# Ordering the rotary queries' split behind two evictions in a four-layer attention trunk

## The chip, the core and the metric

The kernel runs on one core of a Trainium2 chip. The metric is the device time of one execution in microseconds (us); several executions are timed and the median is taken. One further execution is recorded by the hardware profiler.

The engines are called as the profile calls them: PE is TensorE (matmul), PEld its weight load, DVE is VectorE, ACT is ScalarE, POOL is GpSimd, and SP is SyncE, which here only issues transfers.

## The reference

The reference is a decoder trunk of four layers over 256 positions of width 2048, batch 1, all in float32. The layers' token mixers are latent attention (layers 0 and 3), a sparse attention with an indexer (layer 1) and a sliding window (layer 2). The change concerns the latent layers:

```python
c_q, c_kv, k_rope, mq, gate = _split(h @ w_in, [A_Q_LORA, A_KV_LORA, A_ROPE, MEM_WIDTH, BRANCH_WIDTH])
q = (_rmsnorm(c_q, q_norm) @ w_uq).reshape(B, S, A_HEADS, A_NOPE + A_ROPE)      # 16 heads, 128 + 64
kv = (_rmsnorm(c_kv, kv_norm) @ w_ukv).reshape(B, S, A_HEADS, A_NOPE + A_V)     # 16 heads, 128 + 128
q_nope, q_rope = q[..., :A_NOPE], _rope(q[..., A_NOPE:])
k_nope, v = kv[..., :A_NOPE], kv[..., A_NOPE:]
k_rope = _rope(k_rope)                                                          # one for all heads
...
s = (jnp.einsum('bqhd,bkhd->bhqk', qn, k_nope) + jnp.einsum('bqhd,bkd->bhqk', qr, k_rope)) * scale
p = jax.nn.softmax(jnp.where(causal, s, NEG_INF), axis=-1)
return jnp.einsum('bhqk,bkhd->bqhd', p.astype(v.dtype), v)
```

Each layer also attends to 256 memory rows, multiplies the concatenated heads by SiLU of a gate, and adds an output projection to the residual.

## The kernel before

**Numbers in two parts.** A float32 operand is held as a high part, rounded to the format that PE multiplies, and a low part, the difference. A split is one ACT copy (line 58, in the helper `copy_act`) and one DVE subtraction. A product of two split operands is three matmuls: high by high, high by low, low by high. Weights come in pieces of 128 x 1024 by SP's transfers (`wr`), and are split into `wh` (ACT, line 58) and `wl` (DVE, line 72); these splits are kept in the order of the pieces.

**One latent layer.** `Latent.first` makes the latent queries and keys. Then `Latent.project(g)` runs for four groups g of four heads each, followed by `Latent.attend` (scores, softmax, values) and the gate. Over the two latent layers that makes eight groups. Within one group, `project` does, in the order of writing:

1. The rotary queries, `acc_qr`: products by `rows_by`, rotated on DVE, transposed by blocks (`qrT` L457), written to DRAM by POOL (`placed` L463) and read back by four POOL transfers into the tile `qrR` (L473).
2. The latent queries without rotation, `acc_qn`, in two halves of two heads, by `columns_by`. Each half's accumulator is evicted by `head_parts`: an ACT copy of the high part (`qn`, L58), a DVE subtraction (`zl`, L316) and a DVE addition (`qn`, L317).
3. The latent keys, `acc_kn`, in two halves, evicted in the same way. The second half lies in two small accumulators (`apart`), so that `head_parts` takes its other branch: two ACT copies, then L312 and L313 on DVE for each of two heads.
4. The values, `acc_va`, by `rows_by` in two steps of 12 matmuls, s = 0 and s = 2; L266, L267 and L268 are the three products.
5. The function `rotary`, called from a hook of `rows_by` after the matmuls of step s = 0: it splits `qrR` into the tile `qrT`, an ACT copy (L842, seen as L58) and a DVE subtraction on 64 partitions (L843).

`attend` then multiplies the queries by the keys, `sp<-kn,qn`, and the rotary queries by the rotary keys, `sp<-kr,qrT` (both L870).

**Accumulators and buffers.** The large accumulators share two places (`bufs=2`), taken in turn: `acc_qr`, the two halves of `acc_qn`, the first half of `acc_kn`, `acc_va`. So `acc_va` gets the place of the second half of `acc_qn`, as soon as its L317 has ended. The tiles `qrR`, the two `qn` and the two `kn` share five places (`PQ`); `wh` and `wl` have three each.

**What sets the order.** The order of writing is not the order of the engines' queues. A planner goes through a simulated timeline at compile time and puts on each engine the instruction that is ready by its own estimates. Two devices bind it: `tc.keep_in_program_order(x)` keeps marked instructions of an engine in the order of writing among themselves, and `with tc.issue_after(ins)` puts every instruction of the block that runs on the engine of `ins` behind `ins` in that queue. On the chip each queue then runs in the planned order, and an instruction that waits holds up what stands behind it.

## Time and profile before

| | before |
|---|---|
| median of three runs | 2533.45 us (2532.8 to 2538.79) |
| profiled execution: its own time | 2536.98 us |
| profiled execution: span from the first to the last instruction | 2535.2 us |
| mean granted PE clock | 0.998 of full speed |
| busy: PE, DVE, ACT, POOL | 2507.9, 1804.6, 1417.0, 386.0 us |
| busiest pieces of DVE and ACT: the weights' L72, the weights' L58 | 1027.5, 891.3 us |
| moved by transfers | 595.13 MB, mean 235 GB/s |

A line of the timeline gives the start (us from the start of the span), the duration (us), the engine, the line of the kernel, the operation, the tile written and the tiles read, shapes and types, and how many instructions the line merges; a bracket gives the time that the engine stood idle before it and what ended that time. A row of the view by stretches gives the stretch, its length, PE's busy time and number of instructions, the mean granted PE clock, the busy share of the 16 DMA engines and what they moved in GB/s.

The eight groups' `acc_va` start at 535, 623, 713, 804 us (layer 0) and 2114, 2201, 2288, 2377 us (layer 3).

### The profile page before, as it was taken

The page shows a single profiled execution, that of the slowest core. Times are in us where ns is not written, and L with a number is a line of the kernel's source. Part 1 is how long each engine was busy: PE and PEld are TensorE (multiplying, and loading weights), DVE is VectorE, ACT ScalarE, POOL GpSimd, SP SyncE. Part 2 cuts the span into 40 slices and gives each one's busy share as a digit, 9 for nine tenths or more (in the row PEclk, how much of TensorE's full clock was granted, in tenths as well). Part 3 has the DMA queues.
Part 4 walks back from the last instruction along what each step waited for, and adds up shares of the span by engine and source line. Part 5 has one row for each costly group of instructions (what it writes and reads, how often), then busy time and mean ns, then how long its engine had stood idle before and what let it go on. Part 6 is the DMA issues. An engine that isn't in the chain of part 4 may idle for free.

```text
span 2535.2 us, 37192 instructions
## 1 busy us (share of the span) xinstructions
PE 2507.9 (99%) x12868; PEld 2142.0 (84%) x12868; DVE 1804.6 (71%) x3039; ACT 1417.0 (56%) x2240; POOL 386.0 (15%) x615
## 2 busy tenths in 40 slices
PE   8999999999999999999999999999999999999998
PEld 7888888888888888988888888887889888888887
DVE  6555556777767676778888775887887677767677
ACT  6454545554555455656666555666665555545554
POOL 1000001111111110012222201222220111011110
PEclk9999999999999999999999999999999999999999
DMA  9888888977878766679899677999985897788874
GB/s 314 263 280 291 271 261 261 248 202 206 221 201 218 219 190 193 202 230 281 258 281 259 211 213 210 271 270 252 265 235 160 259 240 208 204 225 219 243 207 149
DMA packets 451741, 595.13 MB, mean 235 GB/s; under 512 B 79376, under 2 KB 270496, under 8 KB 450400
## 3 DMA queue, kind: packets, MB, share of 16 engines
q1 hardware_dynamic: 411792, 470.76, 63.5%
q0 software_dynamic: 38752, 121.08, 16.7%
q8 instruction: 102, 1.67, 0.3%
q10 hardware_dynamic: 1008, 0.91, 0.1%
q14 instruction: 87, 0.71, 0.1%
HBM read 535.25 MB, written 69.96 MB: 239 GB/s over the span
## 4 chain that ended last, share of the span: by engine, by line
PE 95%; DMA 2%; DVE 1%; ACT 1%; issue 1%; POOL 0%; SPq 0%; ACTq 0%; DVEq 0%; POOLq 0%
PE acc_mq L290 5%; PE acc_g L290 5%; PE acc_gr L268 4%; PE acc_gr L267 4%; PE acc_gr L266 4%; PE acc_wo L266 4%; PE acc_wo L268 4%; PE acc_wo L267 4%; PE acc_qn L290 3%; PE acc_wo L241 3%; PE acc_wo L239 3%; PE acc_wo L240 3%; PE acc_mq L292 2%; PE acc_g L292 2%; PE acc_mk L267 2%; PE acc_mk L268 2%
## 5 line engine op out<-in xcount | busy, mean ns | idle before, releaser
L72 DVE TENSOR_TENSOR wl<-wr,wh 128x1024 fp32r<-128x1024 f32 (+2 forms) x860 | 1027.5, 1197 | 556.4 <-ACT wh L58 547.8
L58 ACT ACTIVATE wh<-wr 128x1024 fp32r<-128x1024 f32 (+2 forms) x860 | 891.3, 1038 | 840.1 <-PE acc_gr L268 99.4
L267 PE MATMUL acc_gr<-wl,xT 128*128 128x512 f32 x512 | 199.6, 390 | 0.0
L266 PE MATMUL acc_gr<-wh,xT 128*128 128x512 f32 x512 | 199.5, 390 | 0.0
L268 PE MATMUL acc_gr<-wh,xT 128*128 128x512 f32 x512 | 199.5, 390 | 0.0
L266 PE MATMUL acc_wo<-wh,y 128*128 128x512 f32 x432 | 168.8, 391 | 0.5 <-DVE x L1202 0.5
L268 PE MATMUL acc_wo<-wh,y 128*128 128x512 f32 x432 | 168.4, 390 | 0.0
L267 PE MATMUL acc_wo<-wl,y 128*128 128x512 f32 x432 | 168.4, 390 | 0.0
L290 PE MATMUL acc_g<-xT,wh 128*128 128x512 f32 x512 | 162.3, 395 | 0.0
L290 PE MATMUL acc_mq<-xT,wh 128*128 128x512 f32 x512 | 161.8, 396 | 0.0
L577 POOL DMA_DIRECT2D pL<-turn x192 | 120.5, 634 | 210.6 <-DMA turn<-T 92.4
L241 PE MATMUL acc_wo<-wh,y 128*128 128x512 f32 x320 | 124.9, 390 | 0.2 <-DVE y L62 0.2
L240 PE MATMUL acc_wo<-wl,y 128*128 128x512 f32 x320 | 124.9, 390 | 0.1
L239 PE MATMUL acc_wo<-wh,y 128*128 128x512 f32 x320 | 125.0, 390 | 0.0
L1202 DVE TENSOR_TENSOR x<-x,acc_wo 128x1024 f32<-128x1024 f32 x92 | 111.4, 1211 | 16.1 <-PE acc_wo L268 11.4
L290 PE MATMUL acc_qn<-cT,wh 128*128 128x512 f32 x384 | 120.6, 395 | 0.0
L292 PEld LDWEIGHTS acc_g<-xT,wl 128*128 128x128 f32 x512 | 96.0, 188 | 21.7
L292 PEld LDWEIGHTS acc_mq<-xT,wl 128*128 128x128 f32 x512 | 95.1, 188 | 21.1
L267 PEld LDWEIGHTS acc_gr<-wl,xT 128*128 128x128 f32 x512 | 96.2, 188 | 19.3 <-DVE wl L72 0.2
L266 PEld LDWEIGHTS acc_gr<-wh,xT 128*128 128x128 f32 x512 | 96.2, 188 | 19.1
L268 PEld LDWEIGHTS acc_gr<-wh,xT 128*128 128x128 f32 x512 | 96.2, 188 | 19.1
L266 PE MATMUL acc_mv<-wh,mT 128*128 128x512 f32 x256 | 100.7, 394 | 7.3 <-ACT wh L58 7.3
(339 smaller groups left out, 5777.5 us busy)
## 6 DMA issues: line engine op xcount, KB each, us to landing
wr<-in_w_out_dram SPq DMA_DIRECT2D x192, 512.0 KB, 4.9
wr<-in_w_in_a_dram SPq DMA_DIRECT2D x176, 512.0 KB, 4.9
wr<-in_w_mem_kv_dram SPq DMA_DIRECT2D x128, 512.0 KB, 5.8
wr<-in_w_in_b_dram SPq DMA_DIRECT2D x116, 512.0 KB, 4.5
wr<-in_w_in_c_dram SPq DMA_DIRECT2D x104, 512.0 KB, 4.9
wr<-in_w_uq_dram SPq DMA_DIRECT2D x288, 128.0 KB, 3.8
turn<-T POOLq DMA_DIRECT2D x40, 384.0 KB, 5.1
tab<-flat POOLq DMA_DIRECT2D x8, 1536.0 KB, 11.4
```

Source lines behind the costliest of these rows:

```text
L58: return nc.scalar.activation(o, i, AF.Copy, scale=scale)
L72: two = nc.vector.tensor_sub(lo, src, f32(hi))
L239: nc.tensor.matmul(accs[c][:, t], xh, wh[:, at], start=first, stop=False)
L240: nc.tensor.matmul(accs[c][:, t], xh, wl[:, at], start=False, stop=False)
L241: nc.tensor.matmul(accs[c][:, t], xl, wh[:, at], start=False, stop=last)
L266: nc.tensor.matmul(acc[:, t, :n], xh, wh[:, at], start=first, stop=False)
L267: nc.tensor.matmul(acc[:, t, :n], xh, wl[:, at], start=False, stop=False)
L268: nc.tensor.matmul(acc[:, t, :n], xl, wh[:, at], start=False, stop=last)
L290: nc.tensor.matmul(acc[j], wh[:, at[j]], q[:, :, kt % 4, :], start=first, stop=False)
L292: nc.tensor.matmul(acc[j][:, 0, :], wl[:, at[j]], q[:, 0, kt % 4, :], start=False, stop=last)
L577: nc.gpsimd.dma_start(f32(self.raw)[j * 32:(j + 1) * 32, :].rearrange("p (i r) -> p i r", r=r), bass.AP(tensor=d.tensor, offset=d.offset + ...
L1202: nc.vector.tensor_add(xs, xs, acc)
```

## The change

`head_parts` returns its last ACT copy and its last DVE addition. `project` keeps those of the second half of the queries (`ahead`) and of the second half of the keys (`begun`), and `rotary` puts its two instructions behind them, each on its own engine. The hook that calls `rotary` moves from step 0 of the values to step 2.

```diff
         if isinstance(acc, list):
             at = [(dst[:, :, j], z[:, j], acc[j]) for j in range(2)]
             for d, zj, q in at:
-                copy_act(d[:, 0], q[:, 0, :])
+                one = copy_act(d[:, 0], q[:, 0, :])
             for d, zj, q in at:
                 nc.vector.tensor_sub(zj, q[:, 0, :], f32(d)[:, 0])
-                nc.vector.tensor_add(d[:, 1], zj, q[:, 1, :])
-            return
-        copy_act(dst[:, 0], acc[:, :, 0, :])
+                two = nc.vector.tensor_add(d[:, 1], zj, q[:, 1, :])
+            return one.ins, two.ins
+        one = copy_act(dst[:, 0], acc[:, :, 0, :])
         nc.vector.tensor_sub(z, acc[:, :, 0, :], f32(dst)[:, 0])
-        nc.vector.tensor_add(dst[:, 1], z, acc[:, :, 1, :])
+        two = nc.vector.tensor_add(dst[:, 1], z, acc[:, :, 1, :])
+        return one.ins, two.ins
...
                 q = act.tile([P, 2, 2, S], F32R, name="qn", tag="pq", bufs=PQ)
-                head_parts(q, acc)
+                ahead = head_parts(q, acc)
                 qn.append(q)
 
             def rotary():
                 r4 = raw[:].rearrange("p (t m b) -> p m t b", m=4, b=32)
-                tc.keep_in_program_order(copy_act(quads(qr), r4))
-                nc.vector.tensor_sub(quads(qr)[64:], r4[64:], quads(f32(qr))[64:])
+                with ExitStack() as held:
+                    for ins in ahead + begun:
+                        held.enter_context(tc.issue_after(ins))
+                    tc.keep_in_program_order(copy_act(quads(qr), r4))
+                    nc.vector.tensor_sub(quads(qr)[64:], r4[64:], quads(f32(qr))[64:])
...
                 k = act.tile([P, 2, 2, S], F32R, name="kn", tag="pq", bufs=PQ)
-                head_parts(k, acc)
+                begun = head_parts(k, acc)
                 kn.append(k)
             acc = rows_by(self.cT[3:], 4, wkv, 0, (g * 1024, 4, 256, A_NOPE, A_NOPE), "va",
-                          {0: [rotary]})
+                          {2: [rotary]})
```

## The prediction

> **What bounds the kernel now.** I read the page first, for the engine that fills the span and for the chain that ended last.

> ```profile
> span 2535.2 us, 37192 instructions
> PE 2507.9 (99%) x12868; PEld 2142.0 (84%) x12868; DVE 1804.6 (71%) x3039; ACT 1417.0 (56%) x2240; POOL 386.0 (15%) x615
> PE 95%; DMA 2%; DVE 1%; ACT 1%; issue 1%; POOL 0%; SPq 0%; ACTq 0%; DVEq 0%; POOLq 0%
> ```

> TensorE (PE) fills the span but for 27 us, and the chain runs through it. So only time in which PE stands still, or runs slowly, can be won. The view of waits, for PE, says where it stands (waited for: us in total, times, longest).

> ```profile
> PE acc_va L266 <- DVE qn L317: 7.5, 7, 2.9
> PE acc_mv L266 <- ACT wh L58: 7.3, 1, 7.3
> PE acc_va L266 <- ACT kn L58: 1.2, 1, 1.2
> ```

> The first weights of the kernel cost 7.3 us, and nothing in the change touches them. The other large item is the first product of the values, acc_va, which waits eight times, once for each group of the two latent layers. The timeline of PE gives each wait, in the bracket:

> ```profile
> 535.17 0.47 PE L266 MATMUL acc_va<-wh,cT 128*128 128x512 f32 x1 [0.45 <-DVE qn L317]
> 623.19 0.47 PE L266 MATMUL acc_va<-wh,cT 128*128 128x512 f32 x1 [1.16 <-ACT kn L58]
> 712.96 0.76 PE L266 MATMUL acc_va<-wh,cT 128*128 128x512 f32 x1 [2.93 <-DVE qn L317]
> 803.89 0.47 PE L266 MATMUL acc_va<-wh,cT 128*128 128x512 f32 x1 [1.32 <-DVE qn L317]
> 2113.72 0.47 PE L266 MATMUL acc_va<-wh,cT 128*128 128x512 f32 x1 [0.45 <-DVE qn L317]
> 2200.97 0.47 PE L266 MATMUL acc_va<-wh,cT 128*128 128x512 f32 x1 [0.40 <-DVE qn L317]
> 2288.23 0.47 PE L266 MATMUL acc_va<-wh,cT 128*128 128x512 f32 x1 [0.40 <-DVE qn L317]
> 2376.62 0.47 PE L266 MATMUL acc_va<-wh,cT 128*128 128x512 f32 x1 [1.55 <-DVE qn L317]
> ```

> They sum to 8.66 us. Whether such a wait really lengthens the span is seen from one acc_va to the next: span and PE busy time of three such stretches.

> ```profile
> 535.17:623.19 88.02, 86.86 (x472) 1.00 0.77 212
> 623.19:712.96 89.77, 86.84 (x472) 0.99 0.77 208
> 712.96:803.89 90.93, 89.61 (x472) 0.97 0.76 207
> 712.96:718.60 5.64, 5.64 (x13) 0.50 0.64 186
> ```

> The first two hold the same 472 instructions in 86.85 us of PE time; what is left, 1.16 and 2.93, is exactly the wait at their end. The third has 89.61 us: 2.76 more. The last row says why: for 5.64 us after the wait of 2.93 the granted clock (the column behind the count) was 0.50. So the third group costs 2.93 + 2.76 us, and the eight together 8.66 + 2.76 = 11.42 us.

> **Why PE waits there.** acc_va takes the accumulator that the second half of the latent queries, qn, leaves; it is free when VectorE's L317 for that half has ended. In the third group, ScalarE and VectorE:

> ```profile
> 708.05 1.06 ACT L58 ACTIVATE qrT<-qrR 128x1024 fp32r<-128x1024 f32 x1 [2.73 <-DMA qrR<-placed]
> 709.02 0.58 ACT L58 ACTIVATE qn<-acc_qn 128x512 fp32r<-128x512 f32 x1
> 709.14 1.22 DVE L843 TENSOR_TENSOR qrT<-qrR,qrT 64x1024 fp32r<-64x1024 f32 x1 [2.56 <-ACT qrT L58]
> 712.14 0.68 DVE L317 TENSOR_TENSOR qn<-zl,acc_qn 128x512 fp32r<-128x512 f32 x1
> ```

> The rotary split (qrT, one instruction on each engine) stands ahead of the eviction of qn on both queues, and here waits 2.73 us for its transfer qrR. qn's eviction, with all it needs, stands behind it.

> In the first group the transfer was in time, and the split still costs 0.45 us:

> ```profile
> 528.76 0.39 PE L292 MATMUL acc_qn<-cT,wl 128*128 128x256 f32 x2
> 529.01 1.06 ACT L58 ACTIVATE wh<-wr 128x1024 fp32r<-128x1024 f32 x1 [1.73 <-PE acc_qn L290]
> 529.97 1.05 ACT L58 ACTIVATE qrT<-qrR 128x1024 fp32r<-128x1024 f32 x1
> 530.92 0.57 ACT L58 ACTIVATE qn<-acc_qn 128x512 fp32r<-128x512 f32 x1
> 531.35 1.22 DVE L843 TENSOR_TENSOR qrT<-qrR,qrT 64x1024 fp32r<-64x1024 f32 x1
> 531.75 1.06 ACT L58 ACTIVATE wh<-wr 128x1024 fp32r<-128x1024 f32 x1 [0.25 <-PE acc_kn L290]
> 532.61 0.69 DVE L316 TENSOR_TENSOR zl<-acc_qn,qn 128x512 f32<-128x512 f32 x1
> 533.22 1.21 DVE L72 TENSOR_TENSOR wl<-wr,wh 128x1024 fp32r<-128x1024 f32 x1
> 534.33 0.39 PE L292 MATMUL acc_kn<-cT,wl 128*128 128x256 f32 x2
> 534.35 0.68 DVE L317 TENSOR_TENSOR qn<-zl,acc_qn 128x512 fp32r<-128x512 f32 x1
> 535.50 0.64 ACT L58 ACTIVATE kn<-acc_kn 128x256 fp32r<-128x256 f32 x2
> 538.03 0.74 DVE L313 TENSOR_TENSOR kn<-zl,acc_kn 128x256 fp32r<-128x256 f32 x2
> 539.31 1.23 DVE L72 TENSOR_TENSOR wl<-wr,wh 128x1024 fp32r<-128x1024 f32 x1 [0.54 <-ACT wh L58]
> 540.96 0.28 PE L870 MATMUL sp<-kr,qrT 128*128 128x256 f32 x1
> 541.28 0.29 DVE L618 TENSOR_TENSOR u<-sp,caus 128x128 f32<-128x128 f32 x1 [0.75 <-PE sp L870]
> ```

> PE is done with the keys at 534.33 + 0.39 = 534.72 and could start acc_va; L317 ends at 535.03.

> **The change, step by step.** Nothing is added or removed: the same two instructions per group, 1.05 us on ScalarE and 1.22 us on VectorE, move behind the last copies of kn (ScalarE, 535.50 here) and the last L313 (VectorE, 538.03 here). The ordering is the planner's own, within one engine, so it adds no wait between engines; the hook's later place changes only the order of writing. The transfers that fill qrR keep their place in POOL's queue, and SP's queue has no step that is moved.

> *ahead of acc_va, gain.* With the split out of the way ScalarE evicts qn at about 529.97 and VectorE starts L316 at 531.35, where the split starts now; it ends at 532.04. The weights' L72 can't start before its wh ends (531.75 + 1.06 = 532.81), so L317 goes ahead of it and ends by about 532.8, 1.9 us before PE is done at 534.72. If the planner keeps L72 between the two, L317 ends at 532.85 + 1.21 + 0.68 = 534.74, and 0.02 us is left of the 0.45. What is late next is the value weights' own L72: it ends at 532.85 + 1.21 = 534.06, 0.66 us before 534.72, so no wait takes over. The same holds in the other groups, where the qrR transfer no longer stands ahead of anything PE needs. Gain 8.66 us, and 2.76 more where the clock fell.

> *behind acc_va, cost.* ScalarE ends the keys' copies at 536.14 and then idles until its next weights, which wait for PE; the 1.05 us lie in that hole. VectorE ends the last L313 at 538.77 now. Without the split ahead it ends between 537.55 (all of 1.22 us saved) and 538.77 (none, if it waits for the wh pieces instead); I take 538.2, the middle, since some of those waits will show. The split then runs there from 538.2 to 539.45, and at the worst to 540.0. The first rotary product, at 540.96 now and 540.5 after the gain, has 1.05 us to spare, 0.5 at the worst. Behind the split on VectorE stands the gate weights' L72, at 539.31 now and 539.45 then, and the softmax's first L618, which waits for PE by 0.75 us anyway. Cost on the path: nothing; the cover is those 1.05 us. A wait would begin only if VectorE were over 1.05 us later than I put it.

> *the buffer behind the split.* In the fourth and eighth group POOL's load of the memory keys takes qrR's room and waits for L843:

> ```profile
> 801.86 2.30 POOL L473 DMA_DIRECT2D mkr<-mk  x4 [8.75 <-DVE qrT L843]
> 872.25 1.05 ACT L58 ACTIVATE mkh<-mkr 128x1024 fp32r<-128x1024 f32 x1
> ```

> It will start some 6 us later, and is read 70 us after its start now. Cost nothing.

> **The sum.** Against the profiled execution, whose time is 2536.98 (span 2535.2 and 1.78 around it): 2536.98 - 11.42 = 2525.6. The median of the runs shown is 2533.45 (2532.8 to 2538.79), 3.5 us below the profiled execution; the drop of the clock alone, 2.76, would explain most of that. I therefore take it that the median run had the waits and not the slow clock: 2533.45 - 8.66 = 2524.8. With the slow clock in it, 2522.0. A floor for the gain comes from the groups in which the transfer was in time: 0.40 to 0.45 us each, 8 x 0.42 = 3.4 us, if without a profile the transfers are never late: 2530.1.

> [...]

> **The rivals.**
> *Late rotary queries (slower).* The planner puts VectorE's half of the split behind more than I think, say behind the gate weights' L72 and the softmax's first instructions; then the rotary product of the first head stands, and PE with it, which runs in order. Against it: the hole on ScalarE and the 1.05 us to spare. It decides from the point where the wait at that product passes (8.66 + 7.6) / 8 = 2.0 us per group, which is the split ending 3.1 us later than I have it. If it came behind the values' own split, that is 3 to 4 us too late, the loss is 8 x 3.5 = 28 us less the gain: about 2553. Chance 0.07.
> *The lateness is the profile's.* In plain runs the qrR transfer is in time more often, and only 3.4 to 7 us are won: 2526.5 to 2530. For it: the profiled execution is slower than two of three runs. Against it is ScalarE's row among the waits: five of eight splits waited, and not by a hair. Chance 0.22.

> ```profile
> ACT qrT L58 <- DMA qrR<-placed: 6.3, 5, 2.7
> ```

> *No effect.* Another instruction takes the split's place ahead of L317, or VectorE's L72 for the value weights becomes the wait: 2531 to 2535. Against it: nothing else was ready there, and 0.66 us are to spare. Chance 0.10.
> *My forecast*, all eight waits gone: 2522 to 2525.8. Chance 0.61.

> **How the numbers follow.** A difference of 0.3% (7.6 us) is about what a measurement of this kernel tells from no change. Faster by over that (below 2525.9): the forecast, with a little of the partial case, 0.62. Within it: the rest of the partial case, no effect and a small wait instead, 0.30. Slower: 0.08. The range goes from 2520.5 (full gain with the clock, and the 1.5 us by which fast runs differ) to 2531 (the floor, and 1 us); about two in ten lie outside, mostly above.

> **What the next profile would show.** Right: no idle bracket at acc_va, the granted clock at 1.00 in the third group, 86.85 us from one acc_va to the next, and the split on both engines behind the kn copies with no wait for qrR. Wrong: an idle bracket at sp<-kr,qrT; L317 still behind L72 and acc_va waiting; or a new wait anywhere among PE's waits.

## The result and the profile after

The changed kernel takes 2521.07 us (median of four, 2520.52 to 2525.16), the kernel before, run beside it, 2536.12 us (2532.8 to 2540.09): a ratio of 0.9944, 95% interval 0.9923 to 0.9964. The forecast was 2524.8 us, in a range of 2520.5 to 2531. The change made the kernel faster, by some 15 us between these two medians (9 to 20 us by the interval), where the forecast had 8.7 us. The measured time lies 0.6 us above the lower end of the range.

The page of the profile after, in the rows that answer to those of before:

```profile
span 2519.8 us, 37184 instructions
PE 2502.1 (99%) x12868; PEld 2139.8 (85%) x12868; DVE 1804.5 (72%) x3039; ACT 1416.2 (56%) x2240; POOL 385.4 (15%) x615
```

DVE and ACT do the same work as before to within 1 us. The span is 15.4 us shorter, and PE is busy for 5.8 us less. All of PE's waits that are left, in the view of waits:

```profile
PE acc_mv L266 <- ACT wh L58: 7.2, 1, 7.2
PE acc_mv L267 <- DVE wl L72: 1.4, 2, 0.7
PE acc_wo L241 <- DVE y L62: 0.2, 1, 0.2
PE acc_wo L266 <- DVE x L1206: 0.2, 1, 0.2
```

No wait at `acc_va` is among them, and nothing longer than 0.2 us is new. From one `acc_va` to the next (stretch, length, PE busy, count, granted clock), and the first 5.64 us of the third group, which ran at a clock of 0.50 before:

```profile
534.32:620.93 86.61, 86.61 (x475) 1.00 0.81 216
620.93:707.55 86.62, 86.62 (x475) 1.00 0.83 216
707.55:794.17 86.62, 86.62 (x475) 1.00 0.83 216
707.55:713.19 5.64, 5.64 (x28) 1.00 0.65 191
```

Length and busy time are now the same, and the clock is full. Before, these stretches were 88.02, 89.77 and 90.93 us long.

Rows of the first group's timeline after the change, on the three engines:

```profile
528.77 1.06 ACT L58 ACTIVATE wh<-wr 128x1024 fp32r<-128x1024 f32 x1 [1.73 <-PE acc_qn L290]
529.73 0.58 ACT L58 ACTIVATE qn<-acc_qn 128x512 fp32r<-128x512 f32 x1
531.00 0.68 DVE L316 TENSOR_TENSOR zl<-acc_qn,qn 128x512 f32<-128x512 f32 x1
531.72 0.69 DVE L317 TENSOR_TENSOR qn<-zl,acc_qn 128x512 fp32r<-128x512 f32 x1
532.60 1.23 DVE L72 TENSOR_TENSOR wl<-wr,wh 128x1024 fp32r<-128x1024 f32 x1 [0.19 <-ACT wh L58]
534.10 0.39 PE L292 MATMUL acc_kn<-cT,wl 128*128 128x256 f32 x2
534.32 0.40 PE L266 MATMUL acc_va<-wh,cT 128*128 128x512 f32 x1
535.26 0.64 ACT L58 ACTIVATE kn<-acc_kn 128x256 fp32r<-128x256 f32 x2
535.79 1.06 ACT L58 ACTIVATE qrT<-qrR 128x1024 fp32r<-128x1024 f32 x1
537.20 0.74 DVE L313 TENSOR_TENSOR kn<-zl,acc_kn 128x256 fp32r<-128x256 f32 x2
537.97 1.22 DVE L847 TENSOR_TENSOR qrT<-qrR,qrT 64x1024 fp32r<-64x1024 f32 x1
542.59 0.86 PE L874 MATMUL sp<-kr,qrT 128*128 128x256 f32 x6
```

L317 of the queries ends at 532.41, ahead of L72 and 1.9 us before PE wants the accumulator. `acc_va` starts 0.22 us after the last row of the keys (534.32 - 534.10), with no idle bracket. The split stands behind the keys' evictions on both engines, with no wait for its transfer. The rotary products of the first two heads are now together (x6) and come at 542.59, behind seven gate products that the planner put ahead of them; before, the first came at 540.96, ahead of the first gate product.

### The profile page after: what moved, and what is told of

It is laid out like the page before. It is cut to its first block, busy times and chain, and to the rows that moved or that the text cites. A ratio compares the mean times of both kernels' runs of the same rounds, so it can differ in the third digit from the quotient of the medians.

```text
span 2519.8 us, 37184 instructions
## 1 busy us (share of the span) xinstructions
PE 2502.1 (99%) x12868; PEld 2139.8 (85%) x12868; DVE 1804.5 (72%) x3039; ACT 1416.2 (56%) x2240; POOL 385.4 (15%) x615
## 4 chain that ended last, share of the span: by engine, by line
PE 97%; DVE 1%; ACT 1%; DMA 1%; issue 0%; SPq 0%; ACTq 0%; DVEq 0%
PE acc_mq L290 5%; PE acc_g L290 5%; PE acc_gr L266 4%; PE acc_gr L268 4%; PE acc_gr L267 4%; PE acc_wo L268 4%; PE acc_wo L267 4%; PE acc_wo L266 4%; PE acc_qn L290 4%; PE acc_wo L241 3%; PE acc_wo L239 3%; PE acc_wo L240 3%; PE acc_mq L292 2%; PE acc_g L292 2%; PE acc_mk L267 2%; PE acc_q L268 2%
## 5 line engine op out<-in xcount | busy, mean ns | idle before, releaser
L72 DVE TENSOR_TENSOR wl<-wr,wh 128x1024 fp32r<-128x1024 f32 (+2 forms) x860 | 1027.4, 1196 | 550.7 <-ACT wh L58 542.9
L58 ACT ACTIVATE wh<-wr 128x1024 fp32r<-128x1024 f32 (+2 forms) x860 | 891.0, 1038 | 835.4 <-PE acc_gr L268 95.9
L266 PE MATMUL acc_gr<-wh,xT 128*128 128x512 f32 x512 | 199.8, 390 | 0.0
L266 PE MATMUL acc_wo<-wh,y 128*128 128x512 f32 x432 | 168.7, 390 | 0.2 <-DVE x L1206 0.2
L290 PE MATMUL acc_g<-xT,wh 128*128 128x512 f32 x512 | 162.3, 395 | 0.0
L290 PE MATMUL acc_mq<-xT,wh 128*128 128x512 f32 x512 | 161.8, 396 | 0.0
L290 PE MATMUL acc_qn<-cT,wh 128*128 128x512 f32 x384 | 120.6, 395 | 0.0
L292 PEld LDWEIGHTS acc_g<-xT,wl 128*128 128x128 f32 x512 | 96.0, 188 | 21.7
L292 PEld LDWEIGHTS acc_mq<-xT,wl 128*128 128x128 f32 x512 | 95.1, 188 | 21.1
L266 PEld LDWEIGHTS acc_gr<-wh,xT 128*128 128x128 f32 x512 | 96.2, 188 | 18.4
L266 PE MATMUL acc_mv<-wh,mT 128*128 128x512 f32 x256 | 100.7, 393 | 7.2 <-ACT wh L58 7.2
```

The lines of the kernel that those rows point to most:

```text
L58: return nc.scalar.activation(o, i, AF.Copy, scale=scale)
L72: two = nc.vector.tensor_sub(lo, src, f32(hi))
L266: nc.tensor.matmul(acc[:, t, :n], xh, wh[:, at], start=first, stop=False)
L290: nc.tensor.matmul(acc[j], wh[:, at[j]], q[:, :, kt % 4, :], start=first, stop=False)
L292: nc.tensor.matmul(acc[j][:, 0, :], wl[:, at[j]], q[:, 0, kt % 4, :], start=False, stop=last)
```

## The experiments

My theory: what stood ahead of the second half's eviction of the queries, and nothing else, set the time of `acc_va`; the cost was the place of the split itself plus the lateness of its transfer, plus the slow clock behind a long wait. The rivals: the keys' evictions matter too; lateness belongs to the profiled execution only; a split that comes later must make PE wait at the rotary products.

**The hook alone.** Nothing is held; only the hook's step is changed.

```diff
-                          {0: [rotary]})
+                          {2: [rotary]})
```

> Only the hook moves (step 0 to step 2 of the values); nothing is held. In the queues this already puts ScalarE's half of the split behind the queries' eviction (but ahead of both evictions of the keys and of the second piece of the value weights), and VectorE's half behind L317 of the queries. Theory (only the queries' eviction counts, since acc_va takes its accumulator): no wait at acc_va, 13 us less than before, ratio about 0.995. Rival (the keys' evictions must be ahead as well): in the groups where the transfer is 1 to 2.7 us late, ScalarE holds up the second piece of the value weights, PE waits in the middle of acc_va, and 3 to 6 us of the gain are lost: ratio 0.996 to 0.998.

Measured: 2521.77 us against 2534.83 us (15 runs of before), ratio 0.9952 (0.9939 to 0.9964). PE waits nowhere at `acc_va`. Rows of the second group on the three engines:

```profile
616.20 0.58 ACT L58 ACTIVATE qn<-acc_qn 128x512 fp32r<-128x512 f32 x1
618.02 1.06 ACT L58 ACTIVATE wh<-wr 128x1024 fp32r<-128x1024 f32 x1 [1.24 <-PE acc_kn L290]
618.19 0.69 DVE L317 TENSOR_TENSOR qn<-zl,acc_qn 128x512 fp32r<-128x512 f32 x1
618.99 1.04 ACT L58 ACTIVATE qrT<-qrR 128x1024 fp32r<-128x1024 f32 x1
619.94 0.58 ACT L58 ACTIVATE kn<-acc_kn 128x512 fp32r<-128x512 f32 x1
620.37 1.22 DVE L843 TENSOR_TENSOR qrT<-qrR,qrT 64x1024 fp32r<-64x1024 f32 x1
620.84 0.40 PE L266 MATMUL acc_va<-wh,cT 128*128 128x512 f32 x1
```

The split (`qrT`) stands behind the queries' eviction but ahead of the keys', and that is enough. Writing the split later gave the whole gain, without any hold. The first rival is refuted for the lateness that the kernel has.

**The transfer's lateness alone taken away.** The order is that of before; the split reads a tile that has long been there, so the rotary queries are left out of the scores.

```diff
-                r4 = raw[:].rearrange("p (t m b) -> p m t b", m=4, b=32)
+                r4 = x[:, 0, :1024].rearrange("p (t m b) -> p m t b", m=4, b=32)
```

> The kernel before, in which the split reads a tile that has long been there (a part of the residual) instead of the transferred rotary queries, so the rotary part of the scores is replaced; the queues are those of before. It takes away the lateness of the transfer and leaves the order. Theory: every acc_va waits 0.40 to 0.45 us by the brackets (0.6 from start to start), the clock stays at 1.00 in the third group, and 8 us are won (8.66 - 3.4 + 2.76): ratio about 0.997. Rival (lateness belongs to the profiled execution only): the plain runs stay as before, ratio 1.000. Rival (lateness is all): 13 us, ratio 0.995.

Measured: 2528.79 us, ratio 0.9975 (0.9966 to 0.9984). The waits of PE, and two stretches between `acc_va`:

```profile
PE acc_va L266 <- DVE qn L317: 3.3, 8, 0.5
...
622.44:709.66 87.22, 86.82 (x472) 1.00 0.80 215
709.66:796.92 87.26, 86.86 (x472) 1.00 0.82 217
```

All eight waits shrink to 0.40 to 0.46 us, and the clock stays full. Between the medians 6.0 us are won (2534.83 - 2528.79; 4 to 9 us by the interval). The hook alone and the hold alone, below, win 13 us or so in the same set of runs. So lateness with its slow clock makes about half of that, and the order itself the rest. The split of the two is rough: this profile also has 3.6 us of waits of PE in the two middle layers, where the first profile of before has 1.3. The rival that lateness belongs to one profiled execution only is refuted for the timed runs, and so is the one that lateness is all. Every timed run has a span and a granted clock recorded too, so what a wholly unrecorded execution does isn't known.

**The hold alone.**

```diff
 # the change, but:
-                          {2: [rotary]})
+                          {0: [rotary]})
```

> The ordering behind the four evictions alone, with the hook left at step 0. The queues come out the same as with the whole change, so this is also a second measurement of it. Theory: no wait at acc_va, 13 us less than before, ratio 0.994 to 0.995. For the 2.2 us by which the whole change's profile was ahead in the two middle layers, whose queues are the same as before: if they are chance, waits at the third layer's scores and output projection (0.1 to 0.6 us each) come back in this profile or in that of the kernel before, seen again; if the change makes them, they stay away here.

Measured: 2522.27 us, ratio 0.9954 (0.9942 to 0.9967), no wait at `acc_va`. Either part of the change is enough by itself. Its profile has no wait of PE in the two middle layers, apart from 0.2 us at the output projection that is in every profile.

**The kernel before, seen again.**

> The kernel before, profiled a second time. Theory: eight waits at acc_va again, 0.40 to 0.45 us where the transfer is in time and up to 3 us where it is late; the sum may be 6 to 11 us, since the lateness of a transfer differs from run to run, and the clock falls only behind a wait of about 3 us. If lateness is fixed by the program, the waits agree with the first profile within 0.1 us each.

Measured: 2535.67 us, one run. The waits in the third, fourth and sixth group, where the first profile had 2.93, 1.32 and 0.40 us, and the granted clock behind the first two:

```profile
712.44 0.76 PE L266 MATMUL acc_va<-wh,cT 128*128 128x512 f32 x1 [3.64 <-DVE qn L317]
802.77 0.47 PE L266 MATMUL acc_va<-wh,cT 128*128 128x512 f32 x1 [0.93 <-ACT wh L58]
2199.45 0.47 PE L266 MATMUL acc_va<-wh,cT 128*128 128x512 f32 x1 [1.57 <-DVE qn L317]
...
712.44:718.08 5.64, 5.64 (x14) 0.52 0.69 186
802.77:808.41 5.64, 5.64 (x26) 1.00 1.03 263
```

The eight sum to 9.6 us here (8.66 in the first profile): these waits differ from run to run, group by group, by up to 1.2 us, and the slow clock came back behind the longest one.

**More lateness, with the order of before.** The split is called ahead of the eviction of the queries' second half instead of from the hook, and that eviction is held behind it, so that the planner can't put it first. The rotary queries take one more hop through DRAM.

```diff
-            placed(raw[:].rearrange("p (t w) -> p t w", t=8), T, 2)
+            d, size = stored(T)
+            again = dr.tile([2, P, size], F32, name="again", tag="again", bufs=4)
+            nc.gpsimd.dma_start(again, d)
+            fetched(raw[:].rearrange("p (t w) -> p t w", t=8), (again, size), 2, nc.gpsimd.dma_start)
...
-                head_parts(q, acc)
+                with ExitStack() as held:
+                    for ins in rotary() if half else ():
+                        held.enter_context(tc.issue_after(ins))
+                    head_parts(q, acc)
```

> The order of before, written out (the queries' eviction is held behind the split on both engines), with one more hop for the rotary queries: DRAM to DRAM before they are read back, some 4 to 5 us by the landing times of before (3.4 to 5.8 us). More lateness at the same place. Theory: each wait at acc_va grows with the lateness to about lateness plus 0.4 us, 35 to 45 us in all eight; behind each wait of over about 3 us the clock falls to 0.50 and costs some 2.8 us more, in about six groups. Ratio to before 1.015 to 1.025. Rival (the wait in the third group had another cause than the late transfer): little more than before, 1.000 to 1.005.

Measured: 2570.32 us against 2535.8 us (13 runs), ratio 1.013 (1.0111 to 1.015). ScalarE's waits for the transfer, PE's waits, and three stretches behind a wait:

```profile
ACT qrT L58 <- DMA qrR<-again: 36.4, 8, 7.0
...
PE acc_va L266 <- DVE qn L317: 34.1, 6, 7.2
...
625.43:632.00 6.57, 6.57 (x22) 0.74 0.56 162
718.77:726.00 7.23, 7.23 (x20) 0.59 0.52 145
2218.11:2225.00 6.89, 6.89 (x20) 0.64 0.53 152
```

The wait at `acc_va` follows the lateness of the split ahead of it: in each of the six groups PE waits 0.2 us longer than ScalarE does for the transfer (4.32 and 4.13 us in the second group, 7.23 and 7.04 in the fourth). The clock fell in all six. The ratio is a little below what I expected. In the first group of each layer ScalarE waited too, 2.26 and 1.12 us, but PE did not: ScalarE came to the split at 526.98 in the first group, 7.3 us ahead of `acc_va`, and at 616.40 in the second, only 4.7 us ahead of where `acc_va` would start without its wait. The slow clock cost 1.7 to 3.0 us in the three stretches (length times one minus clock), not 2.8 throughout.

**The same hop, with the change, and with the hook alone.** The first part of the diff above (the hop), on the changed kernel and on the kernel with only the hook moved.

> The whole change, with the same additional hop. Theory: the split stands 6 us later in ScalarE's queue than the second half of the queries, so the hop is just covered: no wait at acc_va, 0 to 5 us more than the change alone, ratio to before 0.995 to 0.997. Rival (lateness only moves the wait from acc_va to the gate's first products, which stand behind the split): waits of 1 to 4 us at acc_gr in most groups, ratio 1.000 to 1.010.

> The hook alone moved, nothing held, with the same additional hop. Here the split stands ahead of the keys' evictions and of the second piece of the value weights on ScalarE. Theory: where the transfer is late by over about 2 us that piece is late, and PE waits in the middle of acc_va: 3 to 12 us more than with the evictions held ahead and the same hop. If the holds buy nothing, the two agree within 2 us.

Measured: with the holds 2522.44 us, ratio 0.9945 (0.993 to 0.996); with the hook alone 2534.06 us, ratio 0.9992 (0.998 to 1.0003). With the holds, the ratio is at the lower edge of what I expected. ScalarE waits for the transfer for 0.6 us in all, and PE never for anything in these groups. With the hook alone ScalarE waits for 17.4 us, and PE elsewhere:

```profile
PE sp L873 <- DVE kn L317: 8.2, 4, 2.3
...
PE sp L873 <- ACT va L58: 1.1, 1, 1.1
...
623.00 1.06 ACT L58 ACTIVATE qrT<-qrR 128x1024 fp32r<-128x1024 f32 x1 [3.31 <-DMA qrR<-again]
623.97 0.58 ACT L58 ACTIVATE kn<-acc_kn 128x512 fp32r<-128x512 f32 x1
627.75 0.68 DVE L317 TENSOR_TENSOR kn<-zl,acc_kn 128x512 fp32r<-128x512 f32 x1
628.57 0.47 PE L873 MATMUL sp<-kn,qn 128*128 128x256 f32 x2 [1.96 <-DVE kn L317]
```

The price of 11.6 us between the two is as expected, the place is not. It is the first score that waits, for the eviction of the keys' first half behind the late split, and not the middle of `acc_va`. The rotary product behind it on PE comes at 628.88, though VectorE's half of its `qrT` ended at 625.31 (624.09 + 1.22). So the holds behind the keys buy nothing that these runs show at today's lateness, and nearly the whole gain once the transfer is a hop later.

**The split last of all.** It is held behind the values' own split.

```diff
+            begun = copy_act(v[0], acc).ins, nc.vector.tensor_sub(v[1], acc, f32(v[0])).ins
+            rotary()
```

> The split is held behind the values' own split on both engines, some 3 us later than in the change. This is the slower rival of the prediction, made on purpose. By that rival PE waits 3 to 4 us at the first rotary product, 24 to 32 us in all, ratio to before 1.004 to 1.008 or, with the clock falling, up to 1.015. Theory: the planner, which knows the split to be late, puts gate products ahead of the rotary products on PE (36 of them per group in the queue instead of 7), and PE waits for nothing: ratio 0.994 to 0.996.

Measured: 2522.77 us, ratio 0.9948 (0.9932 to 0.9965), and no new wait. In the first group:

```profile
542.79 0.76 PE L874 MATMUL sp<-kn,qn 128*128 128x256 f32 x5
544.68 1.22 DVE L847 TENSOR_TENSOR qrT<-qrR,qrT 64x1024 fp32r<-64x1024 f32 x1
550.44 0.88 PE L874 MATMUL sp<-kr,qrT 128*128 128x256 f32 x6
```

Counted from the start of `acc_va` (535.59 here, 534.32 with the change), VectorE's half of the split starts 5.4 us later than in the change, and the rotary products come 6.6 us later: the planner filled PE with gate products. So a split that the planner knows to be late doesn't bring the slower rival's loss. A late split with the rotary products kept in their old place on PE was not run.

## Why the prediction was right, and where its sizes were off

The mechanism of the gain was right. The eight waits at `acc_va` were the cost, the split ahead of the queries' eviction was their cause, L317 came out ahead of L72 as forecast (532.41 against 532.8), VectorE's half of the split ended at 539.19 against 539.45 (538.2 + 1.22 gives 539.42), and nothing took over. The load of the memory keys started some 7 us later, counted from the fourth `acc_va` (2.03 us ahead of it before, 5.42 us behind it now), and cost nothing. Which half of the split makes the wait, ScalarE's or VectorE's, was not tried apart.

The cover behind `acc_va` I worked out for a PE queue that stays as it was. The rotary product would have come at about 540.1 (540.96 less the 0.85 by which `acc_va` is earlier), 0.9 us after the split's end at 539.19, where I had 1.05. In fact the planner moved it to 542.59, and 3.4 us were to spare. So the cost came out at nothing as forecast, with more cover than I gave, and luckily so: I had not asked what the planner would do with PE's queue.

Of the sum, one term was too small, one that belonged there was left out, and a part of the difference looks like chance. One statement was wrong. That the time still lies in the range is owed to its lower end, which I had set for the gain with the slow clock and 1.5 us of difference between runs; no run shows the 1.5 us, and the four runs of the changed kernel lie 4.64 us apart (2520.52 to 2525.16).

*The waits themselves.* I summed the idle brackets, 8.66 us. But a stretch without any wait takes 86.62 us, where I read 86.85 us of busy time from the stretches of before: the bracket leaves out 0.23 us at each wait, 8 x 0.23 = 1.84 us in all. Start to start would have shown it: in the first group `acc_va` began 0.84 us after the last row of the keys (535.17 - 534.33) and now 0.22 us after it. That is 0.62 us, where the bracket said 0.45, because it starts only at that row's modelled end, 0.39 us after its start. The rest, some 0.07 us, lies in the first step behind the wait (535.17 to 535.48 before, 534.32 to 534.56 now).

*The slow clock.* I took it out of the median run, on the ground that the profiled execution lay 3.5 us above the median of three. Over 15 runs the median of before is 2534.83 us, and the second profile of before shows the slow clock again. Nine of the 15 runs list a mean granted clock of 0.998 or less and have a median of 2535.84 us; the six at 0.999 have 2532.62. Both profiles with the slow clock list 0.998, the changed kernel's without it 0.999. So most runs seem to have had it, and I should have kept the 2.76 us. With these two, 8.66 + 2.76 + 1.84 = 13.3 us, which is what the timed runs of the three kernels without the waits give (12.6 to 15.1 us).

*The middle layers.* The rest of the 15.4 us between the two profiles is in the main a difference from run to run. From the fourth to the fifth `acc_va` (803.89 to 2113.72 before, 794.17 to 2101.11 after) 2.89 us are saved, of which 0.45 + 0.23 belong to the fifth wait. The other 2.2 us lie where the queues of the two kernels are the same but for the fourth group's scores. The second profile of before takes 1308.27 us for this stretch (802.77 to 2111.04) where the first takes 1309.83. So 1.6 us of the 2.2 differ between two executions of one kernel. The first profile shows two waits there that the second lacks (it has one of 0.39 us elsewhere):

```profile
1743.72 0.38 PE L1056 MATMUL sp<-kd,qS 128*128 128x256 f32 x1 [0.56 <-DVE mn L620]
1753.41 0.47 PE L266 MATMUL acc_wo<-wh,y 128*128 128x512 f32 x1 [0.50 <-DVE x L1202]
```

The same pair of waits came back with the ready source and with the hop on the hook alone. It stayed away with the hold alone, but also with the order of before and more lateness. What decides it in a run was not looked into.

*The hook.* I wrote that its later place changes only the order of writing. In fact it alone gives the gain: with the hook at step 2 the planner put the split behind the queries' eviction on both engines. Why step 0 let the split pass that eviction, which is written still earlier, is open.

*The floor.* A gain of 3.4 us, for a kernel whose transfers are never late without a profile, was no real case: taking lateness away won 6.0 us in the timed runs.

## What to carry to other kernels

Where PE waits for an eviction, look at what stands ahead of it in the evicting engine's queue, and above all at whether that instruction waits for a transfer; an instruction that isn't needed yet belongs behind the ones that give back accumulators (here that took away eight waits, 8.66 us in all). Price such a wait from start to start against a group without it (0.23 us more than the bracket here), and add the slow clock that the trace shows behind the longest one (2.76 us here). Test a new order with a transfer that is made later: two orders that time the same today (0.9952 and 0.9944) came apart by 11.6 us under one more hop.

## What the runs showed of the hardware that was not expected

The granted clock fell to 0.50 behind short waits, and not always behind the longer of two. That it takes a wait of about 3 us was my estimate from the first profile of before, with a fall behind 2.93 us and none behind 1.55 us or less. With the hop on the hook alone it fell behind waits of 1.96 and 2.28 us, and not behind one of 2.32 us.

```profile
626.64:630.05 3.41, 1.48 (x10) 1.00 0.45 124
630.05:633.46 3.41, 3.41 (x11) 0.50 0.63 184
2200.18:2203.60 3.42, 1.84 (x9) 1.00 0.01 4
2203.60:2207.01 3.41, 2.67 (x16) 1.00 0.53 154
2377.68:2381.09 3.41, 1.46 (x7) 1.00 0.57 174
2381.09:2384.50 3.41, 3.08 (x11) 0.50 1.04 269
```

PE was idle for 1.93 us of the step ahead of the first fall and for 1.95 us ahead of the other. The wait of 2.32 us lies in two steps, 1.58 and 0.74 us, and the clock stayed. In the two profiles of before, 1.98 and 2.18 us of a step were idle ahead of the falls, and 1.56 us or less where the clock stayed. So in the groups of these profiles the clock fell where 1.93 us or more of one step were idle, and not at 1.58 us or less; between the two lies no case. All eight waits of 2.93 us and more in the groups had a fall.
